# Strassen factors tied behind the first stage's fixed order, with more buffers for late V tiles and late modulation

## The chip, the cores and the metric

The kernel runs on one core of a Trainium2 chip. The metric is the device time of one execution in microseconds (us), the median over several runs. TensorE (PE) multiplies matrices, VectorE (DVE), ScalarE (ACT) and GpSimd (POOL) work on tiles, and SyncE (SP) issues transfers; ACT issues transfers too. Each engine works through its own row of instructions in order; engines wait for each other, and for transfers, on semaphores.

## The reference

One block over 1024 tokens of 1024 channels, float32. With all rmsnorms over the last axis:

```python
mod = silu(c) @ ada_w + ada_b                       # six sections of 1024: sh1, sc1, g1, sh2, sc2, g2
h = rmsnorm(x, ln1_g) * (1 + sc1) + sh1
q, k, v, cb, cc, cx, ga, gb = split(h @ w_in)       # eight sections of 1024 columns
y_a = stick_breaking_attention(rmsnorm(q), rmsnorm(k), v)      # 16 heads of 64
y_b = cb * causal_dwconv3(cc * cx)
merged = sigmoid(ga) * (y_a @ w_branch_a) + sigmoid(gb) * (y_b @ w_branch_b)
x = x + g1 * (merged @ w_out)
h = rmsnorm(x, ln2_g) * (1 + sc2) + sh2
out = x + g2 * ((silu(h @ w_ffn_gate) * (h @ w_ffn_up)) @ w_ffn_down)
```

In the attention a weight is sigmoid(z) times the product of (1 - sigmoid(z)) over the keys between key and query; a running product along the keys (a scan) gives it.

## The kernel before

Every factor of a product is split into a high and a low part (`whi`, `wlo` for weights), and a product is the sum of three matmul passes. Weights arrive as `raw` tiles of 512 KB; ACT makes `whi`, DVE `wlo`. Most of w_in and the FFN is computed by Strassen's scheme: seven half-size products instead of eight, with sums of weight blocks (`ws`, on POOL) and sums of activation blocks, the factors.

The stages, in order of time:

- Start and first stage, 0 to about 112 us. x is squared for the norm (L245, L246) while the modulation for sh1 and sc1 is summed from `ada` tiles (L233). A silu of c (sigmoid at L248, product at L249) comes ahead of that. For each of eight blocks of channels x is normed (L264), split (`hh`, `hl`: L269, L273) and multiplied (L286). This gives the first half of V, eight tiles: finish_v copies the high part of a tile on ACT (L400), makes the low part on DVE (L401) and stores it to `d_v` on ACT's queue (L402). `vs` has three buffers. The first-stage instructions up to here are kept in the order written by `in_order`, one row per engine. Outside this stretch a planner sets the rows: it may take an instruction that is written later ahead of one that it plans to wait.
- K, about 77 to 182 us: two groups of eight products (`cc` 1 and 2), each followed by finish_k (a square on ACT, a sum, a norming `qn` and a low part on DVE, transposes on PE). Between them a generator `factors()` makes the factors of the later Strassen products from the normed x: 16 steps on DVE (L350, L129), then 16 times an ACT copy (L354), a DVE subtraction into `ts` (three buffers), and a store to `d_t` by SP (L356). After each product two steps of it are written; what is left is written after product (2, 4). Last it stores two parts of `hh` and `hl` to `d_h` from ACT's queue (L370, L371). `ft` is loaded from `d_t` (L435).
- Gates, about 182 to 600 us: 20 Strassen groups of seven products (`g_prod`, PE lines L124 to L126) for q, conv and sigmoid gates, results `c` on DVE. While the gates of sections 3 and 4 run, `mods_later` sums the four later sections of the modulation: 32 tiles of `ada` (L513, ACT's queue), each reduced on DVE (L514). These tiles, the conv tiles `uu` and the row that is sent to `d_g` (L530) share one tag, `uu`, with two buffers.
- Attention, about 600 to 1060 us: scores z (L725, L726), sigmoids on ACT (L727 `pt`, L728 `sg`), the scan on DVE (L732), transposes (L748, L751, L752), products with V (L763). Between its steps PE does other products, the fillers: first the second half of V (L826 to L833, `vs1`, two buffers of tag `ybh`), then the conv branch, whose split results use `ybh` and `ybl`. att_load(h) loads a head (L699 to L702); head 1's is written ahead of the first step.
- The branch and output projections and the FFN, to the end.

Of the kernel before, what the change touches and what calls it, by code (L numbers as in the profile page):

```python
# [8 lines left out]
F32 = mybir.dt.float32  # L9
F32R = mybir.dt.float32r  # L10
# [18 lines left out]
def block_kernel(tc, x, x_t, cols, ada_1, ada_2, ada_row, w_q, w_kv, w_v1, w_cg, w_a, w_b, w_o, w_g, w_u, w_d, out):  # L29
# [117 lines left out]
    def in_order(i0):  # L147

        prev = {}
        for i in nc.cur_bb.bb.instructions[i0:]:  # L150
            if i.engine in prev:
                tc.add_manual_dep(i, prev[i.engine].name,
                                  mybir.DependencyInfo(mybir.DependencyClass.NoSync, mybir.DependencyReason.DATA),
                                  reason="in_order")
            prev[i.engine] = i


    sx = ExitStack()
# [85 lines left out]
    for i in range(8):  # L244
        nc.tensor.matmul(warm, ones, xq[i][:, :512], start=True, stop=True)  # L245
        nc.scalar.activation(xq[i], xq[i], AF.Square, accum_out=ss1[:, i:i + 1])  # L246
        if i == 1:
            nc.scalar.activation(rs, cab, AF.Sigmoid)  # L248
            nc.vector.tensor_tensor(out=cab, in0=cab, in1=rs, op=ALU.mult)  # L249
        if i % 4 == 3:  # L250
            rts.append(rstd_of(ss1[:, i - 3:i + 1], 1.0 / D, sp, 4, eng=nc.vector))
# [155 lines left out]
    for i in (6, 7, 0, 1, 2, 3, 4, 5):  # L407
        mm_tok(pss[i], i, wq, 7, 8)
        finish_v(pss[i], i, 0)
        if i in (0, 2):  # L410
            load_wq(6 + i // 2)
            split_w(6 + i // 2)
    in_order(i0)
    for cc in (1, 2):
        w = wq[4:] if cc == 1 else [load_w(w_kv[cc, j]) for j in range(4)]
        for i in range(8):
            ps = ps_pj()
            mm_tok(ps, i, w, 0, 8)
            while len(tails) >= 2:
                next(tails.pop(0), None)  # L420
            tails.append(finish_k(ps, i, cc - 1))
            next(tails[-1])
            for _ in range(2):
                next(ml, None)
            if (cc, i) == (2, 4):
                for _ in ml:
                    pass
                s2b.close()
                sx.close()
# [69 lines left out]
    def g_big():  # L499
        return gp.tile([P, T + 2], F32, tag="uu", bufs=2, name=nm("uu"))  # L500

    def mods_later():

        csb, cab = g_big()[:, :D], gp.tile([P, D], F32, tag="tr", bufs=2, name=nm("cab"))
        nc.scalar.dma_start(cab, ada_row[0:1, :].broadcast_to([P, D]))
        nc.scalar.activation(csb, cab, AF.Sigmoid)
        tt(nc.vector, cab, cab, csb, ALU.mult)
        yield
        for q, sec in enumerate(SECS):
            ms = gp.tile([P, 8], F32, tag="msum", bufs=2, name=nm("msum"))  # L510
            for k in range(KT):
                ad = g_big()[:, :D]
                nc.scalar.dma_start(ad, ada_2[q, k])  # L513
                nc.vector.tensor_tensor_reduce(out=ad, in0=ad, in1=cab, scale=1.0, scalar=0.0, op0=ALU.mult,  # L514
                                               op1=ALU.add, accum_out=ms[:, k:k + 1])
# [19 lines left out]

    ssq = [g_ss()[:H] for n in range(2)]
    ml = mods_later()
    uu = [g_big() for e in range(2)]
    for e in range(2):
        nc.vector.memset(uu[e][:, :2], 0.0)  # L540
    nss = [0, 0]
    ccs = {}

# [38 lines left out]

    def put_u(c, m, n):

        u = uu[m // 4]
# [192 lines left out]
    def attention():  # L778

        steps = [(h, i) for h in range(H) for i in (LAST if h == H - 1 else ORDER)]  # L780
        for s in range(len(steps) + DAV):
            if s < len(steps):
                h, i = steps[s]
                if s % 8 == 0 and h + 1 < H:
                    with tc.issue_after(lastld[0].ins):
                        att_load(h + 1)
                yield from att_scores(h, i)
            if 0 <= s - 1 < len(steps):
                yield from att_trans(*steps[s - 1])
# [21 lines left out]
    def fillers():  # L811
        for e in range(2):
# [5 lines left out]
            for i in range(8):  # L818
                n, t0 = i // 4, (i % 4) * P
                ps = ps_f()[:, :256]  # L820
                for k in range(KT):
                    if k == 4:
                        yield 1.3
                    wh, wl = (v[:, (k % 2) * 256:(k % 2) * 256 + 256] for v in w[k // 2])
                    sh, sl = hh[n][:, k, t0:t0 + P], hl[n][:, k, t0:t0 + P]
                    nc.tensor.matmul(ps, sh, wh, start=(k == 0), stop=False)  # L826
                    nc.tensor.matmul(ps, sh, wl, start=False, stop=False)
                    nc.tensor.matmul(ps, sl, wh, start=False, stop=(k == KT - 1))
                vs = fq.tile([P, 4, P], F32R, tag="ybh", bufs=2, name=nm("vs1"))
                pv = ps.rearrange("p (h d) -> p h d", d=DH)  # L830
                nc.scalar.activation(vs[:, :, :DH], pv, AF.Copy)
                nc.vector.tensor_tensor(out=vs[:, :, DH:], in0=pv, in1=vs[:, :, :DH].bitcast(F32), op=ALU.subtract)
                nc.scalar.dma_start(d_v[8 + 4 * e:12 + 4 * e, :, i, :].rearrange("h p d -> p h d"), vs.bitcast(F32))  # L833
                yield 1.3
# [552 lines left out]
```

## Time and profile before

| | |
|---|---|
| median of 3 runs | 1919.35 us (1919.15 to 1919.47) |
| profiled execution | 1924.99 us, span 1923.2 us |
| mean granted PE clock | 0.982 of full speed |
| PE busy | 1837.4 us, 96% |
| DVE busy | 1432.4 us, 74% |
| ACT busy | 864.2 us, 45% |
| POOL busy | 431.3 us, 22% |
| moved by transfers | 360.05 MB |

Busy time is time in which the engine works on an instruction; a row of a timeline names the start, the duration, the engine, the line, the operation, and in brackets how long the engine stood before it and on whom. "out<-in" gives the tiles by name. The span is that of one execution; the rest of its time lies before the first and after the last instruction.

### The profile page before, as it was taken

The numbers are of one execution on the slowest core, as the hardware profiler recorded it, in microseconds if no ns is written. First come the engines' busy times: TensorE is split into PE (matmuls) and PEld (weight loads), VectorE is DVE, ScalarE is ACT, GpSimd is POOL, SyncE is SP. The second block draws the span as 40 slices with busy tenths as digits, with TensorE's granted clock in tenths as the row PEclk, the third lists the DMA queues.
The fourth block names the chain that finished last, engine by engine and source line by source line (L and its number), as shares of the span: only waits on it lengthen the run. The fifth ranks groups of instructions, "written<-read, shape, count | busy, mean of one in ns | idle before, by whom it ended". The sixth has DMA issues, their size and how long they took to land.

```text
span 1923.2 us, 24945 instructions
## 1 busy us (share of the span) xinstructions
PE 1837.4 (96%) x8813; PEld 1519.7 (79%) x8813; DVE 1432.4 (74%) x2027; ACT 864.2 (45%) x1602; POOL 431.3 (22%) x317
## 2 busy tenths in 40 slices
PE   7799899999988999998999999989999999999999
PEld 5588677888877888887887788867888888878787
DVE  6953677678684899998999644499988788843954
ACT  4432553333333777776777321464444434422221
POOL 0033236523231000000000000065444445301013
PEclk9899999999999999998999999989999999999999
DMA  9695542225667666659563535323344334389776
GB/s 390 224 360 172 189 154 78 76 82 193 217 230 225 181 170 192 175 179 291 164 164 105 197 130 197 132 82 138 145 171 161 143 142 164 132 312 338 246 230 218
DMA packets 154764, 360.05 MB, mean 187 GB/s; under 512 B 15376, under 2 KB 52496, under 8 KB 152464
## 3 DMA queue, kind: packets, MB, share of 16 engines
q1 hardware_dynamic: 79792, 235.58, 38.0%
q10 hardware_dynamic: 73840, 119.22, 17.5%
q0 software_dynamic: 1008, 3.67, 0.5%
q8 instruction: 70, 1.15, 0.2%
q14 instruction: 54, 0.44, 0.1%
HBM read 243.58 MB, written 114.82 MB: 186 GB/s over the span
## 4 chain that ended last, share of the span: by engine, by line
PE 69%; DVE 15%; DMA 9%; issue 3%; ACT 3%; POOL 1%; ACTq 0%; SPq 0%; DVEq 0%; POOLq 0%
PE e L124 6%; PE e L125 6%; PE e L126 6%; PE pj L124 5%; PE pj L125 5%; PE pj L126 5%; PE pj L286 3%; PE pj L807 3%; PE pj L808 3%; PE pj L809 3%; PE e L1225 3%; PE e L1226 3%; PE e L1224 3%; DVE pt L732 2%; DMA d_v<-vs 2%
## 5 line engine op out<-in xcount | busy, mean ns | idle before, releaser
L732 DVE TENSOR_TENSOR_SCAN pt<-pt,dm 128x256 f32<-128x256 f32 (+7 forms) x128 | 171.5, 1343 | 13.0 <-ACT pt L727 12.6
L115 POOL TENSOR_SCALAR rs_m<-ss 128x1 f32<-128x1 f32 x8 | 1.9, 242 | 663.1 <-ACT xn L1057 663.1
L125 PE MATMUL e<-big,whi 128*128 128x512 f32 x352 | 138.6, 394 | 6.5 <-DVE big L129 6.5
L124 PE MATMUL e<-big,whi 128*128 128x512 f32 x352 | 138.4, 394 | 0.9 <-ACT c L1140 0.9
L126 PE MATMUL e<-big,wlo 128*128 128x512 f32 x352 | 138.0, 392 | 0.0
L727 ACT ACTIVATE pt<-z,rq 128x512 f32<-128x512 f32 (+2 forms) x192 | 112.3, 586 | 45.4 <-PE z L726 19.4
L124 PE MATMUL pj<-big,whi 128*128 128x512 f32 x320 | 126.8, 396 | 4.0 <-DVE c L129 4.0
L125 PE MATMUL pj<-big,whi 128*128 128x512 f32 x320 | 126.6, 396 | 0.0
L1225 PE MATMUL e<-wlo,f 128*128 128x512 f32 (+1 forms) x319 | 122.6, 385 | 3.8 <-DVE wlo L988 3.8
L126 PE MATMUL pj<-big,wlo 128*128 128x512 f32 x320 | 126.1, 396 | 0.0
L129 POOL TENSOR_TENSOR ws<-raw,raw 128x512 f32<-128x512 f32 x41 | 58.0, 1415 | 292.5 <-DMA raw<-w_cg 175.8
L1226 PE MATMUL e<-whi,f 128*128 128x512 f32 (+1 forms) x319 | 122.3, 384 | 0.0
L286 PE MATMUL pj<-whi,big 128*128 128x512 f32 x352 | 112.9, 406 | 9.8 <-DVE vs L401 7.3
L129 DVE TENSOR_TENSOR c<-pj,c 128x512 f32<-128x512 f32 x140 | 93.7, 683 | 35.1 <-PE pj L126 34.6
L1224 PE MATMUL e<-whi,f 128*128 128x512 f32 (+1 forms) x319 | 117.1, 385 | 1.4 <-DMA f<-d_f 1.4
L129 DVE TENSOR_TENSOR c<-e,c 128x512 f32<-128x512 f32 x154 | 102.8, 681 | 20.8 <-PE e L126 20.8
L453 ACT ACTIVATE whi<-raw 128x512 fp32r<-128x512 f32 x116 | 73.0, 632 | 98.6 <-PE pj L125 40.4
L728 ACT ACTIVATE sg<-z,rq 128x512 f32<-128x512 f32 (+1 forms) x192 | 112.2, 587 | 1.1 <-PE tr L748 1.1
L129 DVE TENSOR_TENSOR wlo<-raw,whi 128x512 fp32r<-128x512 f32 x116 | 90.3, 781 | 21.3 <-ACT whi L453 21.0
L752 DVE TENSOR_TENSOR atl<-tr,ath 128x512 fp32r<-128x512 f32 (+1 forms) x192 | 100.5, 543 | 7.1 <-ACT ath L751 6.7
L125 PE MATMUL e<-rl,whi 128*128 128x512 f32 x264 | 102.8, 389 | 1.8 <-DVE rl L129 1.8
L748 PE MATMUL tr<-dm,sg 128*128 128x128 f32 x576 | 93.9, 279 | 10.5 <-DVE atl L752 10.2
(245 smaller groups left out, 5271.5 us busy)
## 6 DMA issues: line engine op xcount, KB each, us to landing
f<-d_f SPq DMA_DIRECT2D x77, 512.0 KB, 4.4
d_f<-fs ACTq DMA_DIRECT2D x70, 512.0 KB, 2.6
raw<-w_cg SPq DMA_DIRECT2D x40, 512.0 KB, 3.9
uu<-ada ACTq DMA_DIRECT2D x32, 512.0 KB, 4.7
raw<-w_g SPq DMA_DIRECT2D x24, 512.0 KB, 3.3
raw<-w_u SPq DMA_DIRECT2D x23, 512.0 KB, 3.3
ada<-ada SPq DMA_DIRECT2D x8, 1024.0 KB, 10.7
d_t<-ts SPq DMA_DIRECT2D x16, 512.0 KB, 5.3
```

Of the source, the lines that this page charges most:

```text
L124: nc.tensor.matmul(ps, wh[:, k, :], fh[:, k, :], start=(k == 0), stop=False)
L125: nc.tensor.matmul(ps, wh[:, k, :], fl[:, k, :], start=False, stop=False)
L126: nc.tensor.matmul(ps, wl[:, k, :], fh[:, k, :], start=False, stop=(k == 3))
L129: eng.tensor_tensor(out=out, in0=a, in1=b, op=op)
L286: nc.tensor.matmul(ps, a, b, start=(k == 0 and q == 0), stop=(k == KT - 1 and q == 2))
L727: nc.scalar.activation(pt[:, off + s0:off + s0 + m], z[:, :m], AF.Sigmoid, scale=rq[:, 1, i, h:h + 1])
L728: nc.scalar.activation(sg[:, s0:s0 + m], z[:, :m], AF.Sigmoid, scale=rq[:, 0, i, h:h + 1])
L732: nc.vector.tensor_tensor_scan(out=pt[:, rev], data0=pt[:, rev], data1=dm[:, rev], initial=0.0, op0=ALU.mult, op1=ALU.add)
L752: nc.vector.tensor_tensor(out=tl[:, :nb, c0:c0 + P], in0=src, in1=th[:, :nb, c0:c0 + P].bitcast(F32), op=ALU.subtract)
L1224: nc.tensor.matmul(o, sh, w[0][:, c], start=(j == 0), stop=False)
L1225: nc.tensor.matmul(o, sh, w[1][:, c], start=False, stop=False)
L1226: nc.tensor.matmul(o, sl, w[0][:, c], start=False, stop=(j == NJ - 1))
```

## The change

1. `in_order` returns the last instructions of DVE and ACT in the fixed stretch, and every step of the factors is written under `issue_after` of both: none of their DVE and ACT instructions may stand ahead of these in the rows. From product (1, 4) on three steps are written per product instead of two, and the rest after (2, 1) instead of (2, 4).
2. The silu of c at the start is written after the sixth square instead of the second.
3. The tiles of the late modulation go round three tags, `uu`, `sq` and `tr`, so that five buffers serve them instead of two; `uu` for the conv is taken only when the conv begins.
4. Head 1's loads are written at the fourth step of head 0 instead of the first.
5. `vs1` goes round `ybh` and `ybl`, four buffers instead of two.

```diff
-    in_order(i0)
+    ends = in_order(i0)          # in_order now returns the last DVE and ACT instruction
+    def more():
+        with tc.issue_after(ends[0]), tc.issue_after(ends[1]):
+            next(ml, None)
...
-            for _ in range(2):
-                next(ml, None)
-            if (cc, i) == (2, 4):
+            for _ in range(2 if (cc, i) < (1, 4) else 3):
+                more()
+            if (cc, i) == (2, 1):
...
-        if i == 1:
+        if i == 5:
             nc.scalar.activation(rs, cab, AF.Sigmoid)
...
-                ad = g_big()[:, :D]
+                tag = ("uu", "sq", "uu", "sq", "tr")[nad % 5]
+                ad = g_big()[:, :D] if tag == "uu" else gp.tile([P, D], F32, tag=tag, bufs=2, name=nm("ad"))
...
-    uu = [g_big() for e in range(2)]
+    uu = []                      # filled in put_u, at the first conv tile
...
-                if s % 8 == 0 and h + 1 < H:
+                if s % 8 == (0 if h else 3) and h + 1 < H:
...
-                vs = fq.tile([P, 4, P], F32R, tag="ybh", bufs=2, name=nm("vs1"))
+                vs = fq.tile([P, 4, P], F32R, tag=("ybh", "ybl")[i % 2], bufs=2, name=nm("vs1"))
```

DVE's row at the end of the first stage, before. `vs` are the low parts of finish_v, `xts` and `ts` rows are factor steps, `wlo` weights:

```order
L216 TENSOR_TENSOR wlo_511<-raw_508,whi_510 128x1024
L350 SCALAR_TENSOR_TENSOR xts<-xts,dsh 128x512
L350 SCALAR_TENSOR_TENSOR xts<-xts,mod 128x512
L401 TENSOR_TENSOR vs_528<-tr_241,vs_528 128x8x64
L350 SCALAR_TENSOR_TENSOR xts<-xts,mod 128x512 x2
L129 TENSOR_TENSOR xts<-xts 128x512
L350 SCALAR_TENSOR_TENSOR xts<-xts,mod 128x512 x2
L401 TENSOR_TENSOR vs_535<-tr_242,vs_535 128x8x64
L350 SCALAR_TENSOR_TENSOR xts<-xts,mod 128x512
L129 TENSOR_TENSOR ts_717<-xts,ts_717 128x512
L129 TENSOR_TENSOR ts_721<-xts,ts_721 128x512
L129 TENSOR_TENSOR ts_725<-xts,ts_725 128x512
```

and with the change:

```order
L217 TENSOR_TENSOR wlo_511<-raw_508,whi_510 128x1024
L402 TENSOR_TENSOR vs_528<-tr_241,vs_528 128x8x64
L402 TENSOR_TENSOR vs_535<-tr_242,vs_535 128x8x64
L402 TENSOR_TENSOR vs_542<-pj_235,vs_542 128x8x64
L217 TENSOR_TENSOR wlo_549<-raw_546,whi_548 128x1024
L402 TENSOR_TENSOR vs_555<-pj_236,vs_555 128x8x64
L402 TENSOR_TENSOR vs_562<-pj_237,vs_562 128x8x64
L217 TENSOR_TENSOR wlo_569<-raw_566,whi_568 128x1024
L402 TENSOR_TENSOR vs_575<-pj_238,vs_575 128x8x64
```

The factor steps have left this stretch; the first of them now stands behind the last `vs`.

DVE's row in the gates where the product `pj_4372` is taken into `c_4364`, before (ISA is the reduction of a modulation tile, in two rows):

```order
L129 TENSOR_TENSOR wlo_4503<-raw_4359,whi_4502 128x512
L514 ISA uu_4471,msum_4147<-uu_4471,cab_3624 128x1024
L514 ISA msum_4147 128x1
L129 TENSOR_TENSOR wlo_4486<-raw_4359,whi_4485 128x512
L129 TENSOR_TENSOR mod<-msum_4147,cst 128x8
L514 ISA uu_4476,msum_4475<-uu_4476,cab_3624 128x1024
L514 ISA msum_4475 128x1
L129 TENSOR_TENSOR c_4364<-pj_4372,c_4363 128x512
```

with the change, around the same `c_4364`:

```order
L129 TENSOR_TENSOR wlo_4429<-ws_4354,whi_4428 128x512
L129 TENSOR_TENSOR wlo_4503<-raw_4359,whi_4502 128x512
L129 TENSOR_TENSOR wlo_4486<-raw_4359,whi_4485 128x512
L129 TENSOR_TENSOR c_4364<-pj_4372,c_4363 128x512
L129 TENSOR_TENSOR wlo_4558<-ws_4519,whi_4557 128x512
L129 TENSOR_TENSOR c_4363<-pj_4338,c_4363 128x512
```

and further up, where the reductions went, three in a row ahead of `c_4198` and `wlo_4335`:

```order
L524 ISA ad_4642,msum_4475<-ad_4642,cab_3624 128x1024
L524 ISA msum_4475 128x1
L524 ISA ad_4648,msum_4475<-ad_4648,cab_3624 128x1024
L524 ISA msum_4475 128x1
L524 ISA uu_4468,msum_4147<-uu_4468,cab_3624 128x1024
L524 ISA msum_4147 128x1
L129 TENSOR_TENSOR c_4198<-pj_4206,c_4197 128x512
L129 TENSOR_TENSOR wlo_4335<-raw_4193,whi_4334 128x512
```

The reductions of the two last sections of the modulation stand here now, earlier; before, one of them stood directly ahead of `c_4198`, and none is left beside `c_4364`.

ACT's row at the start of the attention, before, with what each instruction waits for (DMAHW names a transfer's semaphore); `vs` here are tiles of vs1, numbers two to five:

```order
L831 ACTIVATE vs_965_4926<-pj_4901 128x4x64 [waits PE_49]
L833 DMA d_v<-vs_965_4926 128x4x128 [waits DMAHW5_49,DVE_49]
L831 ACTIVATE vs_967_4955<-pj_4930 128x4x64 [waits DMAHW0_49,PE_49]
L833 DMA d_v<-vs_967_4955 128x4x128 [waits DMAHW1_49,DVE_49]
L831 ACTIVATE vs_969_4984<-pj_4959 128x4x64 [waits DMAHW5_49,PE_49]
L727 ACTIVATE pt_4835<-z_5050,rq 128x256 [waits PE_49]
L727 ACTIVATE pt_4834<-z_5029,rq 128x128 [waits PE_49]
L728 ACTIVATE sg_5028<-z_5029,rq 128x128 [waits DMAHW2_49]
L728 ACTIVATE sg_5049<-z_5050,rq 128x256
L833 DMA d_v<-vs_969_4984 128x4x128 [waits DMAHW6_49,DVE_49]
L831 ACTIVATE vs_971_5013<-pj_4988 128x4x64 [waits DMAHW1_49,PE_49]
```

with the change:

```order
L843 ACTIVATE vs_965_4926<-pj_4901 128x4x64 [waits PE_49]
L845 DMA d_v<-vs_965_4926 128x4x128 [waits DMAHW5_49,DVE_49]
L843 ACTIVATE vs_967_4955<-pj_4930 128x4x64 [waits PE_49]
L845 DMA d_v<-vs_967_4955 128x4x128 [waits DMAHW1_49,DVE_49]
L843 ACTIVATE vs_969_4984<-pj_4959 128x4x64 [waits PE_49]
L739 ACTIVATE pt_4834<-z_5018,rq 128x128 [waits PE_49]
L740 ACTIVATE sg_5017<-z_5018,rq 128x128
L739 ACTIVATE pt_4835<-z_5039,rq 128x256 [waits PE_49]
L740 ACTIVATE sg_5038<-z_5039,rq 128x256
L845 DMA d_v<-vs_969_4984 128x4x128 [waits DMAHW6_49,DVE_49]
L843 ACTIVATE vs_971_5013<-pj_4988 128x4x64 [waits DMAHW0_49,PE_49]
```

The third and fourth `vs` no longer wait for a transfer; the fifth does, for the first one's store.

More of the change, by code (lines that the diff above doesn't have):

```diff
@@ L155, in in_order @@
             prev[i.engine] = i
+        return [prev[e] for e in prev if e in (nc.vector.engine, nc.scalar.engine)]
     sx = ExitStack()
@@ L504, in mods_later @@
         csb, cab = g_big()[:, :D], gp.tile([P, D], F32, tag="tr", bufs=2, name=nm("cab"))
+        nad = 0
         nc.scalar.dma_start(cab, ada_row[0:1, :].broadcast_to([P, D]))
@@ L511, in mods_later @@
             for k in range(KT):
-                ad = g_big()[:, :D]
+                tag = ("uu", "sq", "uu", "sq", "tr")[nad % 5]
+                ad = g_big()[:, :D] if tag == "uu" else gp.tile([P, D], F32, tag=tag, bufs=2, name=nm("ad"))
+                nad += 1
                 nc.scalar.dma_start(ad, ada_2[q, k])
@@ L537, in block_kernel @@
     ml = mods_later()
-    uu = [g_big() for e in range(2)]
-    for e in range(2):
-        nc.vector.memset(uu[e][:, :2], 0.0)
+    uu = []
     nss = [0, 0]
@@ L583, in put_u @@
     def put_u(c, m, n):
+        if not uu:
+            uu.extend(g_big() for e in range(2))
+            for e in range(2):
+                nc.vector.memset(uu[e][:, :2], 0.0)
         u = uu[m // 4]
```

## The prediction

> **What bounds the kernel now.** I read the busy table first, then what TensorE (PE) waited for, then the busy time by stretches, and last the timelines and the chain of waits at the places where the change acts.
>
> ```profile
> PE 1837.4 (96%) x8813; PEld 1519.7 (79%) x8813; DVE 1432.4 (74%) x2027; ACT 864.2 (45%) x1602; POOL 431.3 (22%) x317
> ...
> PE pj L286 <- DVE vs L401: 7.3, 1, 7.3
> ...
> PE pj L826 <- DVE vs L832: 4.5, 1, 4.5
> PE pj L124 <- DVE c L129: 4.0, 1, 4.0
> ...
> PE tr L388 <- DVE qn L382: 0.9, 2, 0.8
> ```
>
> PE is busy 96% of the span, so a gain has to come out of the 86 us in which it stands (1923.2 - 1837.4). The wait rows (total, times, longest) name three long single stops that lie where the diff does: before finish_v's results (7.3), before the later V tiles (4.5), before the gate products (4.0).
>
> ```profile
> 144.00:192.00 48.00, 48.00 (x230) 39.77 (x229) 18.11 (x27) 11.28 (x20) 15.67 (x17) 1.00 0.54 171
> ...
> 672.00:864.00 192.00, 186.60 (x1147) 162.13 (x1146) 188.09 (x279) 148.98 (x321) 0.00 (x0) 1.00 0.64 179
> ```
>
> Each row is a stretch, its length, and the busy time (and count) of PE, PE's weight loads, DVE, ACT and POOL, then clock, DMA share and GB/s. Between the stops PE is full (48.00 of 48 in 144 to 192), so it is the path there: time saved at a stop stays saved. In the attention (672 to 864) VectorE (DVE) is busy 188.09 of 192 and PE 186.60; there both must start earlier for anything to be kept. 48.00/230 gives 0.21 us a matmul, 5.0 us for a product of 24.
>
> **The factors behind the first stage (place A).** 32 DVE steps, 16 ACT copies and 16 SP stores move behind the last of the eight vs. Nothing is removed.
>
> ```profile
> 66.59 2.07 DVE L350 SCALAR_TENSOR_TENSOR xts<-xts,dsh 128x512 f32<-128x512 f32 x3
> 68.58 0.75 DVE L273 SCALAR_TENSOR_TENSOR big<-xts,mod,big 128x512 fp32r<-128x512 f32 x1
> ...
> 74.11 1.22 DVE L216 TENSOR_TENSOR wlo<-raw,whi 128x1024 fp32r<-128x1024 f32 x1
> ...
> 76.57 0.68 DVE L401 TENSOR_TENSOR vs<-tr,vs 128x512 fp32r<-128x512 f32 x1
> 77.17 1.41 DVE L350 SCALAR_TENSOR_TENSOR xts<-xts,mod 128x512 f32<-128x512 f32 x2
> ...
> 84.15 0.68 DVE L401 TENSOR_TENSOR vs<-pj,vs 128x512 fp32r<-128x512 f32 x1
> ...
> 70.65 1.00 PE L286 MATMUL tr<-whi,big 128*128 128x512 f32 x2 [2.42 <-DVE big L273]
> ...
> 84.89 0.80 PE L286 MATMUL pj<-whi,big 128*128 128x512 f32 x1 [7.33 <-DVE vs L401]
> ...
> 70.16 1.06 ACT L215 ACTIVATE whi<-raw 128x1024 fp32r<-128x1024 f32 x1 [1.25 <-DMA raw<-w_kv]
> ...
> 81.56 0.60 ACT L400 ACTIVATE vs<-pj 128x512 fp32r<-128x512 f32 x1 [1.27 <-DVE vs L401]
> ...
> 84.87 0.37 ACTq L402 DMA_DIRECT2D d_v<-vs  x1
> ...
> L124 PE MATMUL pj<-ft,whi x240: 389/394/628, 195.8 to 595.3; 128*128 128x512 f32 x120
> ```
>
> Three factor steps (2.07) stand ahead of the L273 that PE awaits until 70.65, and others ahead of each vs; PE resumes at 84.89, when the third vs (84.15) has freed its bank. Without them DVE is held by the weights: whi at 70.16 to 71.2, wlo (1.22) to about 72.4, first vs by about 73.2. Each further vs takes an ACT copy (0.60), the DVE part (0.68) and the store's issue (0.37), 1.7 us in a row: the third is done at about 76.6 and PE resumes at 76.8, 8.1 earlier. The late queries' 0.9 (qn) goes too, as the first products come earlier than their finish. The matmuls right after such a stop are slow (place B shows rows and a price of 1.5); I count 0.4 of it here.
>
> Where the moved work goes: 32 steps at 0.69 (2.07/3) are 22 us of DVE, 16 copies at 0.60 are 10 us of ACT, over ten products of 5.0 us. finish_k asks DVE for three such operations a product, 2.0; with 2.2 of factors that is 4.2 of 5.0, tight but covered. If that cover goes, the next late thing is qn. SP's stores are now behind the weight loads that they stood among; ten products after 90 the last one leaves near 140. A gate product first reads ft, which is loaded from them, at 195.8, so some 40 us hide the shift. The stores of d_h on ACT's queue move behind d_v's and are read only after the gates: nothing.
>
> The sigmoid at the start moves behind the sixth square.
>
> ```profile
> 10.30 1.04 ACT L248 ACTIVATE rs<-cab 128x1024 f32<-128x1024 f32 x1
> ...
> 11.39 1.12 PE L245 MATMUL pj<-xq,ones 128*128 128x512 f32 x2 [0.15 <-DMA xq<-x]
> ...
> 12.68 1.13 PE L245 MATMUL pj<-xq,ones 128*128 128x512 f32 x2 [0.16 <-DMA xq<-x]
> ```
>
> Without it ACT runs up to the arriving tiles: PE lets go of them at 12.51 and 13.81, ACT would be ready at 12.37 and 13.55. Two gaps, 0.4 us, delay the last square; the ends are 0 (loads bound this stretch) and 1.04. I take 0.4. A is 8.1 + 0.9 + 0.4 - 0.4: -9, with the ends -11 (8.1 + 0.9 + 1.5, rounded) and -4 (rival 1).
>
> **Five buffers for the late modulation (place B).** 32 reductions (L514) stay; their loads may be up to five ahead instead of two.
>
> ```profile
> DVE uu L514 <- DMA uu<-ada: 24.2, 16, 5.5
> ...
> 535.30 2.31 DVE L514 CUSTOM_DVE_ANT_0 uu<-uu,cab 128x1024 f32<-128x1024 f32 x1
> ...
> 552.25 1.22 DVE L514 CUSTOM_DVE_ANT_0 uu<-uu,cab 128x1024 f32<-128x1024 f32 x1 [2.95 <-DMA uu<-ada]
> ...
> 557.37 0.68 DVE L129 TENSOR_TENSOR c<-pj,c 128x512 f32<-128x512 f32 x1
> ...
> 540.51 0.50 PE L126 MATMUL pj<-ft,wlo 128*128 128x512 f32 x1 [1.07 <-DVE wlo L129]
> ...
> 558.20 0.47 PE L124 MATMUL pj<-big,whi 128*128 128x512 f32 x1 [4.00 <-DVE c L129]
> ...
> 559.34 0.63 PE L125 MATMUL pj<-big,whi 128*128 128x512 f32 x1
> ...
> 561.89 0.63 PE L125 MATMUL pj<-big,whi 128*128 128x512 f32 x1
> ...
> 552.27 2.34 POOL L129 TENSOR_TENSOR ws<-raw 128x512 f32<-128x512 f32 x1
> ```
>
> Of DVE's 24.2 us of waits only what ends in a PE stop counts: 4.00 (two reductions and a 2.95 wait stand before the c at 557.37) and 1.07, with seven matmuls 0.42 apart instead of 0.21 (559.34 to 561.89), 1.5. Together 6.6, the upper end. In the new order no reduction is left there; they come earlier, in batches of three and four (3.7 and 4.9 us at 1.22), where wlo is made some products ahead. Zero is the other end; nearest is the stop that vanishes, less a new wait of the 1.07 kind and some: -5.
>
> The row against it: the reduction at 535.30 took 2.31, not 1.22, and POOL's sum at 552.27 took 2.34. The Trainium skill (SBUF — State Buffer, section "Who interferes with whom") says that a DVE operation with two SBUF inputs and a GpSimd operation that reads SBUF hold each other off wholly. The trace agrees as far as these rows go; by that rule every reduction of a batch beside POOL's sums costs a second time, and B gives 0 (rival 2).
>
> **The start of the attention (place C).** Two edits: vs1 gets four buffers, and the loads of head 0 no longer wait for the gate pool's last tile (the buffers fall otherwise).
>
> ```profile
> SPq L699 <- DMA d_g<-uu: 15.6, 1, 15.6
> ...
> 604.05 0.51 SPq L699 DMA_DIRECT2D sqt<-d_q  x1
> ...
> 614.86 0.47 PE L725 MATMUL z<-skh,sqt 128*128 128x128 f32 x2 [2.73 <-issue]
> ...
> 607.39 15.12 DMA d_v<-vs
> 622.60 0.39 ACT vs L831
> 623.01 0.43 DVE vs L832
> ...
> 623.38 1.01 DVE L732 TENSOR_TENSOR_SCAN pt<-pt,dm 128x256 f32<-128x256 f32 x2
> ```
>
> The chain is plain: the fourth vs1 waits 15.12 us for the second one's store, and ACT, in order, holds the first pt behind it, so DVE's first scan comes at 623.38. With four buffers the fourth has no one to wait for; the scan can follow the scores (z) by about 1.4, at 613.5. Head 0's loads start 2 to 9 us before 604.05, so z at 614.86 comes 2.73 earlier. PE saves 2.73 + 4.50 = 7.2 and DVE 9.9; the smaller is kept. The sixth vs1 still waits for that same store; I take 0.7 off for it: -6.5, ends -10 (DVE's lead kept) and -2.5 (rival 3). Head 1's loads are written three steps later, but stand in SP's row where they stood: nothing.
>
> **Sum.** -9 - 5 - 6.5 = -20.5. The profiled execution took 1924.99 us (span 1923.2); the median of the runs is 1919.35, 5.64 less. 1924.99 - 20.5 = 1904.5 profiled, 1898.9 as median.
>
> **Rivals.**
> 1. The first stage waits for its own stores. vs has three buffers, so the fourth waits until the first store (issued near 74) has landed.
>
> ```profile
> DMA to landing us min/median/max: 3.2/8.1/13.3
> ...
> DMA to landing us min/median/max: 3.4/6.0/12.7
> ```
>
> The first row is d_v's stores, the second d_t's. Up to 8.1 the fourth vs is there when PE needs it (about 76.8 + 5.0); at 13.3 PE waits 5 more. A gives 4: 1903.9.
> 2. The batches meet POOL's sums: a batch of three at 2.31 takes 6.9 us and stops PE as before. B gives 0: 1903.9.
> 3. The store of 15.12 was slow because everything loads at once, and the stop only moves to the sixth vs1. C gives 2.5: 1902.9.
> 4. Slower. A ts buffer (three) is free again only when its d_t store has landed, and the copies stand on ACT ahead of finish_k's squares. Two stores a product pass freely while a landing takes under 3 x 5.0/2 = 7.5 us, over the median 6.0. At the longest, 12.7, two take 8.5, PE loses 3.5 a product, 28 over the eight: 1926.9. It decides from 11.3 on (2.56 lost a product).
>
> That the steps do not move is excluded by the order.
>
> **How the numbers follow.** Forecast 0.57; rival 1 0.12; rival 2 0.12; rival 3 0.09; rival 4 0.06; 0.04 for several halves that leave nothing. Below: -11 - 6.6 - 10 = -27.6, 1891.8. Above: rivals 1 and 2 together, -10.5: 1908.9. About 0.2% is what a measurement of this kernel tells from no change. Faster 0.90, same 0.04, slower 0.06.
>
> **What would show it.** A: no factor step of L350 (351 now) on DVE ahead of the last vs, PE's stop of 7.33 under 1.5 and resumption near 77. B: no stop of 4.00 at the products around 558 and DVE's waits for ada well under 24.2. C: first scan some 10 us earlier against the last gate product, no wait of a vs1 over 3 us. Wrong it would be if ACT's ts copies wait for d_t through 90 to 145, if wlo follows a batch with PE standing, or if DVE's lead is lost before 672.

## The result, and the profile after

The changed kernel takes 1887.58 us (median of 4 runs, 1882.65 to 1891.37), the kernel before 1919.41 beside it. The ratio is 0.9822, 95% interval 0.9804 to 0.9839: 31.8 us faster, where 20.5 were forecast, and 4.2 us below the range (1891.8 to 1908.9). A second set of four runs of the same text gave 1889.54 against 1921.17, 31.6 faster. I measure what is taken from the changed kernel against 1888.6, the middle of its two medians.

The profiled execution of after took 1882.65 us (span 1880.9, clock 0.993), the one of before 1924.99 (span 1923.2, clock 0.982). That pair lies 42.3 apart, since before's was 5.6 above its median and after's 4.9 below. Places below are read from the pair; their sizes are some us too large in all.

The busy table and the waits of PE after (total, times, longest):

```profile
PE 1816.5 (97%) x8813; PEld 1507.0 (80%) x8813; DVE 1429.2 (76%) x2027; ACT 864.9 (46%) x1602; POOL 436.0 (23%) x317
...
PE tr L760 <- DVE atl L764: 10.5, 13, 1.8
PE e L125 <- DVE big L129: 8.0, 2, 7.5
...
PE pj L287 <- DVE vs L402: 3.1, 1, 3.1
...
PE pj L124 <- ACT whi L460: 2.3, 1, 2.3
...
PE pj L126 <- DVE wlo L129: 0.9, 1, 0.9
```

The 7.3 is 3.1; the 4.5 of vs1 and the 4.0 of c have left the list. PE stands 64.4 us instead of 85.8, 21.4 less. But the same 8813 matmuls also take 20.9 us less busy time. That half was nearly missing from the forecast. The stretches show it in their clock, first before, then after (columns as in the prediction):

```profile
48.00:96.00 48.00, 35.97 (x138) 27.81 (x139) 43.86 (x69) 19.39 (x30) 0.00 (x0) 0.89 0.64 223
192.00:240.00 48.00, 42.23 (x167) 32.15 (x166) 32.03 (x49) 25.61 (x45) 14.58 (x11) 0.93 0.56 192
528.00:576.00 48.00, 42.93 (x177) 33.80 (x176) 38.57 (x57) 14.97 (x25) 14.66 (x8) 0.96 0.71 235
624.00:672.00 48.00, 44.93 (x324) 42.84 (x324) 41.77 (x63) 36.20 (x80) 0.00 (x0) 0.93 0.60 180
864.00:912.00 48.00, 41.48 (x222) 35.44 (x221) 39.40 (x60) 29.76 (x64) 0.00 (x0) 0.88 0.93 292
```

```profile
48.00:96.00 48.00, 42.31 (x181) 33.32 (x181) 37.60 (x57) 19.41 (x29) 0.84 (x1) 1.00 0.64 200
144.00:192.00 48.00, 45.65 (x208) 37.32 (x207) 17.80 (x29) 10.94 (x19) 14.95 (x15) 0.96 0.91 316
192.00:240.00 48.00, 47.86 (x209) 37.22 (x208) 39.74 (x58) 29.46 (x50) 18.51 (x12) 1.00 0.47 165
528.00:576.00 48.00, 48.00 (x225) 40.02 (x224) 25.09 (x36) 19.04 (x32) 10.09 (x11) 1.00 0.49 165
624.00:672.00 48.00, 48.00 (x347) 44.99 (x346) 46.91 (x70) 38.01 (x84) 0.00 (x0) 1.00 0.66 170
864.00:912.00 48.00, 45.97 (x272) 39.44 (x272) 47.08 (x67) 37.95 (x82) 0.00 (x0) 1.00 0.69 196
```

Where a stop goes, the lowered clock beside it goes too. The rows compare the same times, not the same work, since after runs ahead. The start of the gates is a place that the forecast does not have at all: in 192 to 240 PE gains 5.6 us of work, but after's own stop ahead of the gates (2.35 at 185.16) now falls into 144 to 192, where before was full (48.00, shown in the prediction), so 3.3 are left of the two rows together. A sounder reading follows the same PE instruction, by its number in PE's row, through both timelines: after leads by 7.9 us where PE resumes at place A, by 9.3 at 90, 10.7 from 150 to 195, 16.2 at 235, 18 at 430, 25.6 at 572, 37.6 at 668, 43.5 from 930 and 42.3 at the end. So 10.7 come at place A and in the products right behind it, 5.5 at the start of the gates, 7.5 around place B, 12.0 at place C and some 6 in the stretch 864 to 912.

The timelines of after at places A, B and C:

```profile
72.69 0.68 DVE L402 TENSOR_TENSOR vs<-tr,vs 128x512 fp32r<-128x512 f32 x1
...
76.30 0.69 DVE L402 TENSOR_TENSOR vs<-pj,vs 128x512 fp32r<-128x512 f32 x1 [1.09 <-ACT vs L401]
...
77.04 0.50 PE L287 MATMUL pj<-whi,big 128*128 128x512 f32 x1 [3.11 <-DVE vs L402]
...
89.30 1.42 DVE L351 SCALAR_TENSOR_TENSOR xts<-xts,dsh 128x512 f32<-128x512 f32 x2
...
517.93 2.31 DVE L524 CUSTOM_DVE_ANT_0 uu<-uu,cab 128x1024 f32<-128x1024 f32 x1
...
520.91 0.50 PE L126 MATMUL pj<-ft,wlo 128*128 128x512 f32 x1 [0.93 <-DVE wlo L129]
...
586.51 0.38 ACT L843 ACTIVATE vs<-pj 128x256 fp32r<-128x256 f32 x1 [2.73 <-PE pj L840]
...
587.33 0.43 DVE L744 TENSOR_TENSOR_SCAN pt<-pt,dm 128x128 f32<-128x128 f32 x1
...
595.96 0.33 PE L737 MATMUL z<-skh,sqt 128*128 128x128 f32 x1 [1.57 <-ACT sg L740]
```

A: the first factor step stands behind the last vs, and PE resumes at 77.04 (84.89 before; 76.8 was forecast). B: nothing is left of the 4.00, and only a 0.93 ahead of it, behind a reduction of 2.31. C: no vs1 waits for a transfer, the first scan runs at 587.33 (623.38 before), and the 2.73 of issue is gone.

### The profile page after: what moved, and what is told of

Same layout as the page of the kernel before. It is cut to its first block, busy times and chain, and to the rows that moved or that the text cites. A ratio compares the mean times of both kernels' runs of the same rounds, so it can differ in the third digit from the quotient of the medians.

```text
span 1880.9 us, 24952 instructions
## 1 busy us (share of the span) xinstructions
PE 1816.5 (97%) x8813; PEld 1507.0 (80%) x8813; DVE 1429.2 (76%) x2027; ACT 864.9 (46%) x1602; POOL 436.0 (23%) x317
## 3 DMA queue, kind: packets, MB, share of 16 engines
q10 hardware_dynamic: 73840, 119.22, 17.7%
## 4 chain that ended last, share of the span: by engine, by line
PE 72%; DVE 15%; DMA 5%; ACT 4%; issue 2%; POOL 1%; ACTq 0%; SPq 0%; DVEq 0%; POOLq 0%
PE e L124 7%; PE e L125 7%; PE e L126 7%; PE pj L124 5%; PE pj L126 5%; PE pj L125 5%; PE pj L287 5%; PE pj L819 4%; PE pj L820 3%; PE pj L821 3%; PE e L1237 3%; PE e L1238 3%; PE e L1236 3%; DVE pt L744 3%; PE tr L760 2%
## 5 line engine op out<-in xcount | busy, mean ns | idle before, releaser
L744 DVE TENSOR_TENSOR_SCAN pt<-pt,dm 128x128 f32<-128x128 f32 (+7 forms) x128 | 171.5, 1344 | 6.0 <-ACT pt L739 5.5
L739 ACT ACTIVATE pt<-z,rq 128x512 f32<-128x512 f32 (+1 forms) x192 | 112.7, 587 | 40.9 <-PE z L738 17.8
L129 POOL TENSOR_TENSOR ws<-raw,ws 128x512 f32<-128x512 f32 x62 | 98.3, 1585 | 22.4 <-DVE wlo L1000 20.7
```

The lines of the kernel that those rows point to most:

```text
L129: eng.tensor_tensor(out=out, in0=a, in1=b, op=op)
L739: nc.scalar.activation(pt[:, off + s0:off + s0 + m], z[:, :m], AF.Sigmoid, scale=rq[:, 1, i, h:h + 1])
L744: nc.vector.tensor_tensor_scan(out=pt[:, rev], data0=pt[:, rev], data1=dm[:, rev], initial=0.0, op0=ALU.mult, op1=ALU.add)
```

## The experiments

Each kernel was run side by side with the kernel before (medians 1919.3 to 1921.2). The verdict is in the ratio to it and the ratio's interval, and a gain in us is what the ratio lacks to 1, times 1919.4.

### Parts alone

**The factors' tie (edit 1) alone.**

```diff
-    in_order(i0)
+    ends = in_order(i0)
...
-            for _ in range(2):
-                next(ml, None)
+            for _ in range(2 if (cc, i) < (1, 4) else 3):
+                more()               # next(ml) under issue_after(ends[0]), issue_after(ends[1])
```

> Before with the factors' tie and pace alone (edit 1). Two theories share that PE stands 9 us less between 66 and 111 us. 'Stops and clock': each stop also costs the half-speed matmuls behind it, so the clock of 48 to 96 rises from 0.89 to about 1.0 and the median falls by 9 to 12 (1907 to 1910). 'Stops alone' (the forecast's counting): 8 to 9 (1910 to 1911), and the stops at 195.8, 203.4 and 228 remain under both. Rival 'this edit brings the rest too' (its stores and loads reach the gates in another way): over 20 us, and the stop at 203.4 is gone.

1909.22 us, ratio 0.9946 (0.9929 to 0.9964): -10.4. PE resumes at 76.13 here. A is as large as forecast, and it is edit 1's alone; it lies in the range of 'stops and clock' (9 to 12), but its interval (6.9 to 13.6) does not exclude 'stops alone' (8 to 9).

```profile
76.13 0.80 PE L287 MATMUL pj<-whi,big 128*128 128x512 f32 x1 [3.02 <-DVE vs L402]
...
193.48 0.63 ACT L460 ACTIVATE whi<-ws 128x512 fp32r<-128x512 f32 x1 [6.40 <-DMA d_k<-khl]
193.52 1.31 DVE L129 TENSOR_TENSOR wlo<-ws,whi 128x512 fp32r<-128x512 f32 x2 [6.24 <-DMA d_k<-khl]
```

The last two rows are at the start of the gates: ACT and DVE wait over 6 us for the last store of the keys to `d_k`, and PE stops behind them (2.05). This wait is also in before:

```profile
195.83 0.50 PE L124 MATMUL pj<-ft,whi 128*128 128x512 f32 x1 [2.27 <-ACT whi L453]
...
202.65 0.63 ACT L453 ACTIVATE whi<-ws 128x512 fp32r<-128x512 f32 x1 [6.88 <-DMA d_k<-khl]
202.69 1.31 DVE L129 TENSOR_TENSOR wlo<-ws,whi 128x512 fp32r<-128x512 f32 x2 [6.71 <-DMA d_k<-khl]
203.44 0.50 PE L126 MATMUL pj<-ft,wlo 128*128 128x512 f32 x1 [2.53 <-DVE wlo L129]
```

**`uu` taken late, alone** (half of edit 3).

```diff
-    uu = [g_big() for e in range(2)]
-    for e in range(2):
-        nc.vector.memset(uu[e][:, :2], 0.0)
+    uu = []                      # the same lines run in put_u, at the first conv tile
```

> Before with only the conv tiles uu taken at first use (two lines of edit 3); the modulation keeps two buffers. Theory 'layout': the pool's tiles fall on other addresses, so the gates' first wlo no longer wait for the last d_k store (6.9 us on ACT at 202.65) and head 0's loads no longer for d_g: PE's stops of 2.53 at 203.4, 0.97 at 228 and 2.73 at 614.9 go, with slow matmuls behind them some 8 to 10 us less (1909 to 1911). Rival 'five buffers': without more buffers nothing moves, 1918 to 1920, the stop at 203.4 stays.

1907.91 us, ratio 0.9933 (0.9916 to 0.9951): -12.9, the largest part by its median (its interval overlaps that of edit 1), and more than the 8 to 10 of 'layout'. PE's order is that of before in all 8813 matmuls. The start of the gates in its timeline:

```profile
194.74 1.67 ACT L453 ACTIVATE whi<-ws 128x512 fp32r<-128x512 f32 x3
195.40 1.90 DVE L129 TENSOR_TENSOR wlo<-ws,whi 128x512 fp32r<-128x512 f32 x3 [2.06 <-ACT whi L453]
...
195.94 0.50 PE L124 MATMUL pj<-ft,whi 128*128 128x512 f32 x1 [2.27 <-ACT whi L453]
```

Three whi run in a row and wait for no transfer; the stop of 2.53 is gone. After shows the same (whi at 183.96, three in a row, 1.67). The 2.73 of issue at head 0 goes as well, as the forecast had it for the loads, but alone that gives little there: the stop for vs1 grows from 4.50 to 5.26.

PE's order being the same, the gain can be followed matmul by matmul. This kernel leads before by nothing at 190, by 4.9 us at 205, 9.3 at 545 and 11.9 at 615. The first step is the stop and two stretches of lowered clock that before has at 197 and 204. The second is a pace: between 240 and 500 both kernels run the same 624 matmuls on `big`, and each takes 4 ns less here (shortest, median and longest in ns; one of three rows alike, before first, `uu` late second):

```profile
L124 PE MATMUL pj<-big,whi x208: 387/393/506, 248.0 to 499.0; 128*128 128x512 f32 x104
L124 PE MATMUL pj<-big,whi x208: 389/389/500, 243.2 to 491.6; 128*128 128x512 f32 x104
```

From start to start they lie 231 ns apart at the median in all seven kernels with `uu` early, and 227 in all eleven traces with `uu` late; over the 900 such matmuls of the gates that is 3.6 us. The last part is the 2.73 at head 0. So the waits at the start are less than half of the 12.9. Why `big` is read faster was not tried.

**Five buffers (the other half of edit 3) alone.**

```diff
-                ad = g_big()[:, :D]
+                tag = ("uu", "sq", "uu", "sq", "tr")[nad % 5]
+                ad = g_big()[:, :D] if tag == "uu" else gp.tile([P, D], F32, tag=tag, bufs=2, name=nm("ad"))
```

> Before with only the modulation tiles on three tags (the other lines of edit 3). Theory 'layout': the stops at 540.5 and 558.2 go (5.1, with 1.5 to 3 of slow matmuls: 6 to 8 us less, 1911 to 1913), those at 203.4 and 614.9 stay. Rival 'five buffers': 14 us or more, and the stop at 203.4 goes. Forecast's term: 5 us.

1916.99 us, ratio 0.9982 (0.9968 to 0.9995): -3.5, about half of what 'layout' gave it (6 to 8). The 4.00 is gone, a 0.72 for wlo is left. The stop of 4.00 is not the same in every kernel with two buffers: it measured 0.97 to 4.74 us in the seven of them.

**vs1 on four buffers (edit 5) alone, head 1's loads (edit 4) alone, and both.**

```diff
-                if s % 8 == 0 and h + 1 < H:
+                if s % 8 == (0 if h else 3) and h + 1 < H:          # edit 4
...
-                vs = fq.tile([P, 4, P], F32R, tag="ybh", bufs=2, name=nm("vs1"))
+                vs = fq.tile([P, 4, P], F32R, tag=("ybh", "ybl")[i % 2], bufs=2, name=nm("vs1"))   # edit 5
```

> Before with only four buffers for vs1 (edit 5). 'Stops and clock': the stop of 4.50 at 623.5 goes, and with it the slow matmuls from 623.5 to 627 and the following stop of 2.41 at 656.9: 7 to 10 us less (1909 to 1912). 'Stops alone': 4.5 (1915). Rival 3 of the forecast (the store is slow anyway, the stop moves to the sixth vs1): under 2 us.

> Before with edit 4 alone. 'Pair': nothing to repair, within 2.5 us of before. 'Edit 4 by itself': 5 to 10 us less, since undoing it cost 8.

> Before with edits 4 and 5 together. 'Pair': edit 5 alone changes PE's row in the attention in over a thousand places, with edit 4 the row keeps before's pattern; together they give the stop of 4.50 at 623.5, its slow matmuls and the 2.4 at 656.9, 6 to 9 us less than before (1910.5 to 1913.5). 'Singles': edit 5's 2.9 and nothing from edit 4, 1916 to 1917.

Edit 5 alone: 1917.53, ratio 0.9985 (0.9972 to 0.9999), -2.9. Edit 4 alone: 1918.35, ratio 0.9991 (0.9977 to 1.0005), nothing that can be told from zero. Both: 1909.93, ratio 0.9945 (0.9928 to 0.9963), -10.6. So the two are no sum. Edit 5 alone fell short of 'stops and clock' (7 to 10) and the pair went a little over its 6 to 9. Two stops of PE in the timeline of the kernel with edit 5 alone:

```profile
663.99 0.63 PE L748 MATMUL tr<-dm,sg 128*128 128x128 f32 x4 [0.91 <-DVE sg L734]
...
737.89 0.44 PE L748 MATMUL tr<-dm,sg 128*128 128x128 f32 x2 [1.61 <-DVE atl L752]
```

The 4.50 is gone there (1.13 is left in its place), but at 564 places of PE's 8813 another matmul stands than in before (compared by tiles and shape): the planner orders the steps of the heads anew, and stops of 0.8 to 1.6 come up through the heads, these two among them. Its lead over before grows by 6.5 us from 615 to 668 and shrinks again by 4.6 up to 850. With edit 4 beside it only 133 places differ (75 with edit 4 alone), the old rhythm stays, and the lead grows by 6.3 us from 615 to 668 and is kept.

### The change without one part

**Without `uu` late.** The reverse of that diff.

> The changed kernel without the two lines that take the conv tiles uu at first use; everything else, the five modulation buffers too, is kept. 'Layout': the gates' first wlo wait again for the last d_k store and head 0's loads for d_g; PE's stops of 2 to 2.5 near 194 and of 2 to 3 before the first scores are back, with slow matmuls: 9 to 13 us over the changed kernel (1897 to 1901, ratio to before 0.988 to 0.990). 'Five buffers carry edit 3': within 3 us of the changed kernel (0.982).

1896.73, ratio 0.9885 (0.9863 to 0.9906): 8.1 slower than the changed kernel, a little under the 9 to 13 of 'layout', with the ratio inside it. The wait for the keys' store is back:

```profile
191.45 0.63 ACT L460 ACTIVATE whi<-ws 128x512 fp32r<-128x512 f32 x1 [5.52 <-DMA d_k<-khl]
191.49 1.32 DVE L129 TENSOR_TENSOR wlo<-ws,whi 128x512 fp32r<-128x512 f32 x2 [5.35 <-DMA d_k<-khl]
```

**Without four buffers for vs1; without edit 4; without five buffers; without edit 2.** Each has its lines as in before.

> The changed kernel with vs1 back on two buffers (edit 5 undone). 'Stops and clock': the fourth vs1 waits again for the second one's store, PE stands 4 to 5 us there and 2 us near the first products with V, with slow matmuls behind: 6 to 9 us over the changed kernel (1894 to 1897). By what edit 5 gave alone (2.9 with an interval of 0.2 to 5.4): 1890 to 1891.

> The changed kernel with head 1's loads written ahead of the first step again (edit 4 undone). The forecast costed this edit at nothing: within 3 us of the changed kernel. Rival: the planner's rows of the attention differ from there on (ACT takes the second score tile ahead of the first), and PE stands 1 to 4 us more before it.

> The changed kernel with the modulation tiles back on two buffers, the conv tiles still taken late. The stops at 540 and 558 of before are back (4 to 5 us and slow matmuls): 4 to 7 us over the changed kernel (1891.5 to 1894.5). If edit 3 is addresses alone, within 2.

> The changed kernel with the silu of c after the second square again (edit 2 undone). Forecast: the edit costs 0.4, its ends are 0 and 1.04. The changed kernel's second group of transposes at the start began at 20.71 against 19.98 before; undone it begins near 20.0, and 0.3 to 1 us less stands in the rows up to 60 us. The median should move less than it can tell.

| without | us | ratio | interval | against 1888.6 |
|---|---|---|---|---|
| `uu` late | 1896.73 | 0.9885 | 0.9863 to 0.9906 | +8.1 |
| four buffers for vs1 | 1893.81 | 0.9865 | 0.9852 to 0.9879 | +5.2 |
| head 1's loads later | 1895.71 | 0.9881 | 0.9864 to 0.9898 | +7.1 |
| five buffers | 1892.40 | 0.9850 | 0.9832 to 0.9868 | +3.8 |
| sigmoid later | 1889.07 | 0.9838 | 0.9824 to 0.9851 | +0.5 |

By the ratios, against 0.983 for the changed kernel, the five are 10.6, 6.7, 9.8, 3.8 and 1.5 us; that they differ from the last column by up to 3 shows how far one such number can be trusted. The sigmoid's step can't be told from nothing. Five buffers came inside the times given ahead; four buffers for vs1 lie between the two numbers given ahead; head 1's loads are far over the 3 us that went with the forecast. Without edit 4 another matmul stands at 659 places of PE's row, and the stops for sg grow from 7.0 us in after to 10.7; two rows of its timeline:

```profile
598.72 0.79 PE L737 MATMUL z<-skh,sqt 128*128 128x512 f32 x1 [2.91 <-ACT sg L740]
...
854.00 0.58 PE L737 MATMUL z<-skh,sqt 128*128 128x256 f32 x1 [3.76 <-ACT sg L740]
```

In the pair of profiles it is behind by 2.2 us before the first z already (its stop ahead of the gates was 4.21 long, after's 2.35), by 14.3 at 930 and by 12.6 at the end. Without the five buffers PE's order is that of after, and the old stop stands there, with its slow matmuls:

```profile
536.99 0.76 PE L124 MATMUL pj<-big,whi 128*128 128x512 f32 x1 [3.70 <-DVE c L129]
537.55 0.63 PE L125 MATMUL pj<-big,whi 128*128 128x512 f32 x1
```

The same kernel's row of the stretch has the clock of before again, 0.93 where after has 1.00:

```profile
528.00:576.00 48.00, 44.30 (x182) 35.79 (x181) 35.27 (x55) 16.34 (x27) 13.90 (x12) 0.93 0.72 244
```

### What a stop costs beyond itself

To price the slow matmuls, the changed kernel gets a stop in the middle of the gates, where PE was full: PE transposes a tile that DVE has just written two (or seven) times more. The product of the transpose is not used.

```diff
+        with tc.issue_after(hold[0]) if hold else ExitStack():   # later products stand behind it
             half_prod(ps, w, *fac[q])
...
+        if g == 8:
+            for _ in range(2):        # 7 in the second kernel
+                nc.vector.tensor_tensor(out=c21, in0=c21, in1=ones[:, :1].broadcast_to([P, 512]), op=ALU.mult)
+            hold.append(nc.tensor.transpose(g_bank()[:, :P], c21[:, :P], ident).ins)
```

> The changed kernel with one extra PE instruction in the ninth gate group (a transpose whose result nobody reads) that waits for three DVE operations instead of none: a stop of 1.8 to 2.6 us put into a stretch in which PE never stands. Price of a short stop. 'Stops alone': the matmuls behind it stay 0.23 apart, and the later rows come as much later as the stop is long. 'Stops and clock': some matmuls behind it are 0.43 apart, up to 1.7 us on top; by the stops of 3.1 and 2.4 us seen in the changed kernel's rows without slow matmuls, I expect none here.

> The same with eight DVE operations: a stop of 5.2 to 6 us. 'Stops and clock': about eight matmuls behind it are 0.43 apart instead of 0.23, 1.6 to 1.8 us more, so the rows behind come 7 to 7.8 later. 'Stops alone': 5.2 to 6 and no slow matmul.

Both stops came out longer than designed, 6.20 and 11.16, since the added operations queued behind others on DVE. The design (a stop under 3 us) was thus missed, but two prices are there. The stop of 2.4 in the changed kernel (2.35 at 185.16), which the first expectation takes to be without slow matmuls, has six of them behind it. The timeline of the first:

```profile
354.98 0.48 PE L663 MATMUL pj<-dm,c 128*128 128x128 f32 x1 [6.20 <-DVE c L662]
355.11 0.77 PE L124 MATMUL pj<-ft,whi 128*128 128x512 f32 x1
355.68 0.63 PE L125 MATMUL pj<-ft,whi 128*128 128x512 f32 x1
...
359.10 0.42 PE L124 MATMUL pj<-ft,whi 128*128 128x512 f32 x1
```

and of the second:

```profile
361.49 0.48 PE L663 MATMUL pj<-dm,c 128*128 128x128 f32 x1 [11.16 <-DVE c L662]
...
362.19 0.63 PE L125 MATMUL pj<-ft,whi 128*128 128x512 f32 x1
...
367.31 0.54 PE L125 MATMUL pj<-ft,whi 128*128 128x512 f32 x1
367.68 0.39 PE L126 MATMUL pj<-ft,wlo 128*128 128x512 f32 x1
```

The matmuls start 0.43 apart instead of 0.23, for 3.99 us (355.11 to 359.10) and 6.07 us (361.61 to 367.68), so about 2.0 and 3.0 us are lost beyond the stops. The rows behind come later by as much: from 300 to 430 the two kernels fall behind after by 8.4 and 14.3 us, for 8.2 and 14.2. Their single executions took 1893.02 and 1902.70, 4.4 and 14.1 above 1888.6; executions of one kernel spread by 7 to 9 us, so these two tell less than the rows.

### A better order of the first stage

The 3.11 that is left at A is vs's round trip (copy, low part, store's issue). Here the store of a tile is issued after the next tile's copy.

```diff
-        nc.scalar.dma_start(d_v[...], vs.bitcast(F32))
+        store_v()                                   # issues the store kept from the tile before
+        late.append((d_v[...], vs.bitcast(F32)))
```

> The changed kernel with finish_v's store written one tile later on ACT's queue, so that the next copy needn't wait behind a store that waits for DVE. If the 1.8 us a vs (copy, DVE part, issue) sets PE's remaining stop of 3.1 at 77, it falls to about 1.2: 2 us less than the changed kernel (1885 to 1887). Rival: the third vs is held by the weights' wlo, the stop stays, 0. Second rival: the moved rows of the factors bring a new wait of qn or of the ts copies, 1 to 4 more.

> The changed kernel with finish_v's store one tile later and the silu after the second square: the stop at 77 falls by 1.8 as in the run with the later store alone, and the start by 0.3 to 1. If saved stops stay saved, 2 to 3 us under the changed kernel (1884.5 to 1885.5); if something later takes them back, as the median of the run with the later store alone (1887.04) lets one think, 1886 to 1889.

1887.04, ratio 0.9831 (0.9806 to 0.9855), and with the sigmoid back in its old place 1885.80, ratio 0.9819 (0.9806 to 0.9833). The stop shrinks from 3.1 to 1.3 and 1.2:

```profile
PE pj L287 <- DVE vs L408: 1.3, 1, 1.3
```

No median can be told from the changed kernel's, so what the shorter stop saves is not shown in the time. Lastly the changed kernel itself once more:

> The changed kernel once more, word for word: 1885 to 1890 as median; PE's stops of more than 1 us at the same places as in its first profile, and the mean clock between 0.987 and 0.993, with which the single times go (1891 at 0.987, 1883 at 0.993).

1889.54 (1886.11 to 1893.53), ratio 0.9838 (0.9817 to 0.9858). PE stands 65.3 us in its profile, nearly after's 64.4; a kernel's executions differ roughly with their mean clock (1882.65 at 0.993, 1886.95 and 1888.21 at 0.991, 1891.37 at 0.987 in the first set; 1886.11 and 1889.45 at 0.992, 1889.62 at 0.991, 1893.53 at 0.987 in the second).

## Why the prediction was right in sign and short in size

The time fell below the whole range. Two terms that the prediction put at nothing carry most of what is missing: what the late `uu` changes outside head 0's loads, and edit 4. A third, the matmuls at half the pace behind the stops, was counted too small.

**A, forecast -9: right.** -10.4 alone, resumption at 77.04 against 76.8. "1.7 us in a row" for each vs is 1.8 in the rows (72.69, 74.52, 76.30). One sign was set too strictly: "PE's stop of 7.33 under 1.5" came true only with the later store of the pipelined kernel (1.3); 3.11 was left, since PE also came to the stop earlier. The 0.21 us a matmul (48.00/230) mixes shapes: matmuls of 512 columns start 0.23 apart, so a product takes some 5.4 and not 5.0, which changes no term.

**B, forecast -5: about right.** -3.5 alone, 3.8 when taken away. DVE's waits for ada fell from 24.2 to 1.5 (0.9 and 0.6 in its two kinds of tile). The 1.07 became 0.93, as "a new wait of the 1.07 kind" allowed. Rival 2 came in a small part: of the 32 reductions eight took 1.63 to 2.31 us, each while POOL was summing; most took 1.21. One of them, 2.31 at 517.93, stands directly ahead of the wlo that PE waits 0.93 for. The rule of the Trainium skill on DVE and GpSimd (SBUF — State Buffer, "Who interferes with whom") shows in these rows, and by them it cost under 1 us of the 5.

**C, forecast -6.5: right in mechanism, too small.** Edits 4 and 5 gave -10.6 without the loads of head 0 being freed. The step that failed here is "Head 1's loads are written three steps later, but stand in SP's row where they stood: nothing". It looked at SP's row alone. The point at which the loads are written also enters the planner's row of the attention for PE, and with edit 5 but without edit 4 that row is another, with stops through the heads; in the changed kernel the edit is worth 7.1 us (9.8 by the ratio). Edit 4 alone gives 1.7 (interval 4.4 faster to 1.0 slower), edit 5 alone 2.9, both 10.6. PE's row had to be compared too, and under each edit by itself. The end "-10 (DVE's lead kept)" was nearest; 7.2 "PE saves" was the choice that lost, and rival 3 did not happen.

**The missing term, and the largest step that failed.** "The loads of head 0 no longer wait for the gate pool's last tile (the buffers fall otherwise)" was followed to head 0 only. The same edit gives 12.9 us alone, of which only the 2.73 of those loads stood in the sum. It takes away the waits of 6.88 and 6.71 for the keys' store at 202.65, worth 5 us in the profiles with the lowered clock behind them, and it shortens the matmuls on `big` in the gates, 3.6 us. The rows stood in before's trace ahead of the forecast (a second and third stop within 8 us, clock 0.93 in the stretch), but none of the places it looked at was there. That the tiles taken later leave other places in the pool to the first whi and wlo, which no longer lie where the stored keys lay, is argued from the rows: ACT's whi waits 4.5 to 7.4 us for the keys' store in the kernels with `uu` early, and at most 1.1 in those with `uu` late. The faster `big` fits it too. The addresses themselves are not shown by any run.

**The slow matmuls.** They were counted as 0.4 (A) and 1.5 (B). At A alone the lead grows from 7.9 where PE resumes to 9.3 at 90. Of matmuls of 512 columns that start 0.38 to 0.48 apart there are 79 in before and 38 in after (51 in its second profile). Before has fourteen at A, seven behind the stop at 195.83, seven behind 203.44, seven at 558 and eleven in 881 to 913; at these places after has only six, behind its stop at 185.16. At 0.2 us each the difference is 8 of the 20.9 us of busy time. The granted clock tells the rest: it was 0.50 for 68 us in before and 27 in after, and PE worked for 58 and 23 of them. Half of that is lost, 29 and 11.5 us, so 17.7 of the 20.9. Part of it is the executions' own spread (27 and 31 us at 0.50 in the two profiles of the changed kernel); between medians, as an estimate, 31.8 - 21.4 leaves about 10.

**The sum.** Alone, the parts give 10.4 + 12.9 + 3.5 + 10.6 = 37.4; together 31.7. The 6 us between them are no more than the intervals of the four allow, so whether the parts overlap stays open. In place of the forecast's 9 + 5 + 6.5 stand 10.4 (A), 3.5 to 3.8 (B), 10.6 (edits 4 and 5) and 8.1 to 12.9 (`uu` late). Rival 1 (vs waiting for its own stores) and rival 4 did not come: `d_v` landed in 4.2 to 6.3 us in the first stage, and ACT waited 0.5 us for ts in all. Rival 4 rested on a row read wrongly: 3.4/6.0/12.7 holds five loads from `d_t` beside the sixteen stores. The stores alone landed in 3.4 to 9.4 us in before (median 5.3) and in 3.1 to 8.5 in after (4.9), all under the rival's point of 11.3.

Still open: the stretch 864 to 912, some 6 us in the profile pair, where before has stops of 3.35 and 2.08 with eleven slow matmuls and after 1.69 and 1.32 with none. No edit touches it; several of the experiments show the slow group there (without edit 4, without `uu` late), others not, and the second profile of the changed kernel has its clock lowered there too (868 to 871).

## What to carry to other kernels

When an edit changes when a pool's tile is taken, list every instruction before and after it whose waits change, over the whole program, and look in the trace at each one that waited for a transfer: the stop that went with the largest gain stood 100 us ahead of the first use of the tile that is taken later, and some 350 ahead of the modulation that the edit was meant for. When a planner sets the order, two edits can be worth nothing apart and ten us together, so compare the rows under each alone. A stop of PE of 4 to 11 us cost 1.4 to 3.0 more behind it here, in matmuls at half the pace; one of 2 to 3 us cost between nothing and 2.6, by where it fell (next section).

## What the runs showed of the hardware

A stop can be followed by matmuls at about half the pace (0.43 for 0.23 us), for a time that does not follow the stop's length simply: about 4.0 us after 6.20, 6.1 after 11.16. The stop at A was 3.02 and 3.11 long in two kernels, and only the 3.02 was followed by slow matmuls. The granted clock explains both. In all 18 profiles it is 1.00 or 0.50, and within one profile it changes only on a grid of 3.41 us: in before it falls at 197.23, 204.06 and 559.04, which are 2 and 104 steps apart. Where the grid lies differs from execution to execution. Two steps of it around the stop at A, in after and then in the kernel with edit 1 alone (columns as before, PE's work first, its clock third from the right):

```profile
72.40:75.81 3.41, 1.54 (x7) 0.94 (x5) 1.66 (x3) 0.74 (x2) 0.00 (x0) 1.00 0.63 180
75.81:79.22 3.41, 2.18 (x9) 1.80 (x10) 1.39 (x2) 2.00 (x3) 0.00 (x0) 1.00 1.13 343
```

```profile
72.09:75.50 3.41, 1.02 (x5) 0.52 (x3) 1.17 (x3) 1.19 (x2) 0.00 (x0) 1.00 0.66 199
75.50:78.91 3.41, 2.78 (x7) 2.23 (x8) 1.88 (x3) 1.54 (x2) 0.00 (x0) 0.50 1.15 346
```

In after the grid cuts the stop in two, and PE stands 1.87 us in the first step. In the other kernel it stands 2.39, and the clock falls. After's stop of 2.35 at 185.16 lay in one step too (it stands 2.23 of 181.63 to 185.04) and was followed by 0.50. Over the 18 profiles, from 30 us on, all 94 steps at full clock in which PE stood 2.0 us or more were followed by a step at 0.50, none of the 9377 under 1.4, and 40 of the 152 between. The clock came back after a step in which PE stood under 0.45 us (129 of 129), and not after 0.6 or more (56 of 56). So the slow time is what is left of the step in which PE resumes, and one more step if PE stood long in that one.

The Trainium skill (TensorE: Matmul & The Clock Gate, Part 1) says that the clock is halved after an idle window of about 3.4 us, that the window runs freely, and that the slow time is therefore variable. The grid of 3.41, its free place and the half pace agree; that the whole window is idle was not needed here, 2.0 us of it were enough, and the measurement decides.

In before the second and third stores of vs1 took 15.12 and 12.62 us to land, in after the first six took 4.45 to 7.47, with the same bytes. What held them up was not tried by itself.
